# Loading projection weights and kept outputs one step ahead in a hybrid attention layer

## The chip, the cores and the metric

One Trainium2 chip, one core. The metric is device microseconds of one execution of the whole layer, as the median of several runs.

## The reference, cut to what matters

A streaming-encoder layer: 1024 tokens, width 1024, batch 1, float32. Its mixer runs eight heads of multi-head latent attention (MLA: low-rank latents, up projections to queries, keys and values, norms, rope) beside eight heads of chunked attention; one output projection takes both.

```python
q  = rmsnorm(q_lat, g_q) @ w_q_up                  # 256 -> 8 heads x 96
kv = rmsnorm(kv_lat, g_kv) @ w_kv_up               # 128 -> 8 heads x (64 keys + 64 values)
q, k = rmsnorm(q, g_mla_q), rmsnorm([k_nope, k_rope], g_mla_k)
o_mla = mla_attention(rope(q), rope(k), v)         # chunk-causal softmax
o_ca  = chunk_attention(cq, ck, cv, rel_bias)      # band of 9 chunks of 64
mixed = concat(o_mla, o_ca) @ w_out                # 1024 x 1024
x = x + g_a * mixed
x = x + g_m * (silu(gate) * val) @ w_down          # causal convolution and gated MLP, width 2816
```

## The kernel before

**Number form.** A float32 operand of a matrix product is kept as a high part in the matmul's own float32 form and a low remainder. One product is three matmuls: high x high (L150), high x low (L151), low x high (L152). So each weight that is loaded is *split*: a copy makes the high part (`hi_of`, L75, mostly on ACT), a subtraction the low part (`lo_of`, L82, on POOL or DVE).

**Stages.** Up to about 400 us the kernel does norms, input projection and the chunked heads; up to about 656 us the MLA heads' attention; to about 745 us the output projection, gated residual and norm; then the MLP.

**Units and fillers.** Attention is written as *units*: one head and one half of the tokens, eight tiles of 128 queries for both halves. The chunked heads have names with `c` (`Pc`, `hlc`, `PTc`, `pvc`), the MLA heads names with `m`. A tile's scores (L658) go through exp on ACT (L683, into `P`), the scaling to fp16 pairs on POOL (`hl`, L71) and DVE (L703), a DMA transpose issued by SP (`PT`, L705) and the values' matmuls (`pv`, L716). A finished half is scaled (`sb`, L723, and `o`, L724) and stored to `oT_d` in DRAM (L725). Between the tiles' steps the program takes pieces of a list of *fillers*, in this order: values and query/key projections of the chunked heads, `f_m` (the latents, tokens by tiles of 128), `f_up(0)` and `f_up(1)` (the up projections of the first and second four MLA heads) and `f_oca`. A pace (1.9 in chunked, 0.5 in MLA units) sets how much filler work follows each tile. `f_oca` multiplies the chunked heads' outputs, read back from `oT_d`, by their half of the output weights: two column halves n of 512, eight token tiles t in each; its results go to `part_d`. After the last unit, the other half of the output weights (rows 0 to 511, MLA) is loaded, and a loop over eight token tiles (`op` matmuls, kept outputs `ol`/`oh` L876, gate row `gabc` L872, stored partial sum `pa` L882 and L887, gate L888, residual add L889, `x1_d` L890) finishes the projection.

**Order.** All engines work their instructions in order. The order on each engine is decided at build time by the tile framework's scheduler, which runs its own model of the engines: an instruction written later moves ahead on its engine when its inputs and its buffer are free and the engine would be idle in the model. Scores, softmax and values have raised priority. So buffers decide how far ahead a load can be issued. SP issues all DMAs around the change, transposes included, in one queue.

**Buffers.** `qtile` gives one of two `sq` buffers (128 x 512 float32), `rtile` one of four `R` buffers. The chunked heads' values `vts` lie in six buffers of tag `v16`, which are free when the chunked units that read them are done. Split weights go to `G4`, eight buffers. In before:

- `f_up(gr)`: two query weights `wqr` (DMA L526) and the key/value weight `wkr` (L532) go through `sq` and are split to `wq`, `wk`; `wkj` (L535) is a sum of squares of it. Then for each token tile: `qu` matmuls, `uqr` (L553), `usq` (L555), `uss`, the power that makes the norm factor (L115, L116 on POOL), `qn` (L561), rope on POOL (L467 to L470); `ku` matmuls, `kraw` (L569), `vt` (L571, L572), `kss`, `kn` (L581, L582).
- `load_wo(k0, n, he, le)` (L586): four row blocks of the output weights for column half n, each loaded to `sq` (`wor`, L591) and split to `wo`. `f_oca` calls it for k0 = 4 at the start of each n; the line ahead of the projection calls it for k0 = 0 and both n, with the low part on POOL for n = 0 and on DVE for n = 1.
- `f_oca` loads a token block of kept outputs to `cl` (L604), copies the high part to `ch` and subtracts on POOL, and multiplies.

Of the kernel before, what the change touches and what calls it, by code (L numbers as in the profile page):

```python
# [12 lines left out]
F32 = mybir.dt.float32  # L13
# [49 lines left out]
def layer_kernel(ctx, tc, I, out):  # L63
# [3 lines left out]
    def f32(ap):  # L67
        return ap.bitcast(F32)
# [403 lines left out]
    def f_m():  # L472
        w = load_w("wm_", I["w_m"], NM)
        lat = {}
        for t in range(NT):
            h, j = divmod(t, 4)
            sl = slice(j * P, (j + 1) * P)
            pt = ps.tile([P, 512], F32, name=f"mp_{t}", tag="mm", bufs=2)
            yield from gemm3_f(pt[:, :NM], [(hT[k, h][:, 0, sl], hT[k, h][:, 1, sl]) + w[k] for k in range(ND)])
            raw = rtile(f"lat_{t}")  # L480
            act.activation(raw[:, :NM], pt[:, :NM], AF.Copy)
            sq = qtile(f"msq_{t}")
            ss = cst.tile([P, 2], F32, name=f"mss_{t}", tag="ss", bufs=4)
            r = cst.tile([P, 2], F32, name=f"mr_{t}", tag="rr", bufs=4)
            act.activation(sq[:, :QR], raw[:, :QR], AF.Square, accum_out=ss[:, 0:1])
            act.activation(sq[:, QR:QR + KVR], raw[:, QR:QR + KVR], AF.Square, accum_out=ss[:, 1:2])
            act.activation(sq[:, QR + KVR:NM], raw[:, QR + KVR:NM], AF.Square, accum_out=ssr[:, t:t + 1])
            pool.tensor_scalar(ss[:, 0:1], ss[:, 0:1], 1.0 / QR, EPS, op0=MUL, op1=ADD)
            rsqrt_mean(r[:], ss[:], KVR, cols=slice(1, 2))
            pool.tensor_scalar(raw[:, :QR], raw[:, :QR], r[:, 0:1], 1.0, op0=MUL, op1=MUL)  # L490
            pool.tensor_scalar(raw[:, QR:QR + KVR], raw[:, QR:QR + KVR], r[:, 1:2], 1.0, op0=MUL, op1=MUL)
            rope_apply(kr[:, t:t + 1, :], raw[:, QR + KVR:NM].unsqueeze(1), tabk, t, 1, raw[:, NM:NM + 64])
            lat[t] = raw
            if j == 3:
                for b in range(3):
                    ptt = ps.tile([P, 512], F32, name=f"lt_ps{h}_{b}", tag="T", bufs=TB)
                    for jj in range(4):
                        pe.transpose(ptt[:, jj * P:(jj + 1) * P], lat[4 * h + jj][:, b * P:(b + 1) * P], ident[:])
                    pg = pgtile([P, 2, 512], F32R, f"latT{h}_{b}")
                    gain = pk[:, C_GQL + b:C_GQL + b + 1]  # L500
                    act.activation(pg[:, 0], ptt[:], AF.Copy, scale=gain)
                    dve.scalar_tensor_tensor(pg[:, 1], ptt[:], gain, f32(pg[:, 0]), op0=MUL, op1=SUB)
                    latT[b, h] = pg
                    yield 436
# [9 lines left out]

    mq, mk, mv = {}, {}, {}

    def f_up(gr):
        if gr == 0:
            right.__exit__(None, None, None)
            for i in "4v3":  # L520
                G["cm" + i] = tc.tile_pool(name="gp" + i, bufs=1, side="right", reuse_waits="tile")
                G[i] = G["cm" + i].__enter__()
        wq = []
        for k in range(2):
            raw = qtile(f"wqr{gr}_{k}")
            sp.dma_start(raw[:, :384], I["w_qu"][gr][:, k, :])  # L526
            w = g4([P, 2, 512], F32R, f"wq{gr}_{k}")
            hi_of("a", w[:, 0, :384], raw[:, :384])
            lo_of("p", w[:, 1, :384], raw[:, :384], w[:, 0, :384])
            wq.append(w)  # L530
        raw = qtile(f"wkr{gr}")
        sp.dma_start(raw[:], I["w_kvu"][gr])  # L532
        ssw = cst.tile([P, 1], F32, name=f"sswm{gr}")
        junk = qtile(f"wkj{gr}")
        act.activation(junk[:, 0:256].rearrange("p (a b) -> p a b", a=4),  # L535
# [6 lines left out]
        for t in range(NT):  # L542
            h, j = divmod(t, 4)
            sl = slice(j * P, (j + 1) * P)
            if t % 2 == 0:
                mq[gr, t // 2] = g3([P, 2, 4, QK], F32, f"qn{gr}_{t}")
                mk[gr, t // 2] = g3([P, 2, 4, QK], F32, f"kn{gr}_{t}")
                mv[gr, t // 2] = G["v"].tile([P, 2, 4, 2, 64], F16, name=f"vt{gr}_{t}", tag="Gv", bufs=8)
            pt = ps.tile([P, 512], F32, name=f"qu{gr}_{t}", tag="mm", bufs=2)
            yield from gemm3_f(pt[:, :384], [(latT[k, h][:, 0, sl], latT[k, h][:, 1, sl], wq[k][:, 0, :384], wq[k][:, 1, :384])  # L550
                                for k in range(2)])
            raw = rtile(f"uqr{gr}_{t}")
            act.activation(raw[:, :384], pt[:, :384], AF.Copy)  # L553
            sq = qtile(f"usq{gr}_{t}")
            act.activation(sq[:, :384], raw[:, :384], AF.Square)  # L555
            ss = cst.tile([P, 4], F32, name=f"uss{gr}_{t}", tag="ss", bufs=4)
            r = cst.tile([P, 4], F32, name=f"ur{gr}_{t}", tag="rr", bufs=4)
            dve.tensor_reduce(ss[:], sq[:, :384].rearrange("p (a b) -> p a b", a=4), axis=AX.X, op=ADD)
            rsqrt_mean(r[:], ss[:], QK)
            q_t = mq[gr, t // 2][:, t % 2]  # L560
            dve.tensor_tensor(q_t, raw[:, :384].rearrange("p (a b) -> p a b", a=4),  # L561
                              r[:].unsqueeze(2).to_broadcast([P, 4, QK]), op=MUL)
            rope_apply(q_t[:, :, NOPE:], q_t[:, :, NOPE:], tabq, t, 4, raw[:, 0:256])
            pt = ps.tile([P, 512], F32, name=f"ku{gr}_{t}", tag="mm", bufs=2)
            yield from gemm3_f(pt[:], [(latT[2, h][:, 0, sl], latT[2, h][:, 1, sl], wk[:, 0], wk[:, 1])])
            p4 = pt[:].rearrange("p (a b) -> p a b", a=4)
            raw = rtile(f"kraw{gr}_{t}")
            r3 = raw[:, :256].rearrange("p (a b) -> p a b", a=4)
            act.activation(r3, p4[:, :, 0:NOPE], AF.Copy)  # L569
            v_t = mv[gr, t // 2][:, t % 2]  # L570
            act.activation(v_t[:, :, 0, :], p4[:, :, NOPE:], AF.Copy, scale=sc)  # L571
            dve.scalar_tensor_tensor(v_t[:, :, 1, :], p4[:, :, NOPE:], sc, v_t[:, :, 0, :], op0=MUL, op1=SUB)  # L572
            s3 = raw[:, 256:512].rearrange("p (a b) -> p a b", a=4)
            act.activation(s3, r3, AF.Square)
            ss = cst.tile([P, 4], F32, name=f"kss{gr}_{t}", tag="ss", bufs=4)
            r = cst.tile([P, 4], F32, name=f"kr{gr}_{t}", tag="rr", bufs=4)
            dve.tensor_reduce(ss[:], s3, axis=AX.X, op=ADD)
            pool.tensor_tensor(ss[:], ss[:], ssr[:, t:t + 1].to_broadcast([P, 4]), op=ADD)
            rsqrt_mean(r[:], ss[:], QK)
            k_t = mk[gr, t // 2][:, t % 2]  # L580
            dve.tensor_tensor(k_t[:, :, 0:NOPE], r3, r[:].unsqueeze(2).to_broadcast([P, 4, NOPE]), op=MUL)  # L581
            pool.tensor_tensor(k_t[:, :, NOPE:], kr[:, t:t + 1, :].to_broadcast([P, 4, ROPE]),  # L582
                               r[:].unsqueeze(2).to_broadcast([P, 4, ROPE]), op=MUL)


    def load_wo(k0, n, he, le):  # L586
        ws = []
        for k in range(k0, k0 + 4):
            raw = qtile(f"wor{k}_{n}")
            sl = slice(n * 512, (n + 1) * 512)  # L590
            sp.dma_start(raw[:], I["w_out"][k * P:(k + 1) * P, sl])  # L591
            w = g4([P, 2, 512], F32R, f"wo{k}_{n}")
            hi_of(he, w[:, 0], raw[:])
            lo_of(le, w[:, 1], raw[:], w[:, 0])
            ws.append(w)
        return ws

    def f_oca():
        for n in range(2):
            ws = load_wo(4, n, "a", "p")  # L600
            for t in range(NT):
                lo = rtile(f"cl{t}_{n}", (P, 4, P), F32R)
                hi = rtile(f"ch{t}_{n}", (P, 4, P), F32R)
                sp.dma_start(f32(lo[:]), oT_d[4:8, :, t * P:(t + 1) * P].rearrange("k p t -> p k t"))  # L604
                hi_of("a", hi[:], f32(lo[:]))
                lo_of("p", lo[:], f32(lo[:]), hi[:])
                pt = ps.tile([P, 512], F32, name=f"oc{t}_{n}", tag="mm", bufs=2)
                yield from gemm3_f(pt[:], [(hi[:, k], lo[:, k], ws[k][:, 0], ws[k][:, 1]) for k in range(4)])
                o = qtile(f"co{t}_{n}")
                act.activation(o[:], pt[:], AF.Copy)  # L610
                sp.dma_start(part_d[t][:, n * 512:(n + 1) * 512], o[:])


    def qk_page(src, name, rows, tag, bufs, gain):
# [218 lines left out]

    wo = [load_wo(0, n, "a", "v" if n else "p") for n in range(2)]
    att.__exit__(None, None, None)
    att_pg.__exit__(None, None, None)
    psA.__exit__(None, None, None)
# [312 lines left out]
```

## Time and profile before

| | us |
|---|---|
| median of three runs | 1465.47 |
| the three runs | 1463.65, 1468.99, 1465.47 |
| the profiled execution | 1464.36 |
| its span | 1462.2 |
| TensorE busy | 1278.0 (87%) |
| VectorE (DVE) busy | 1013.6 (69%) |
| GpSimd (POOL) busy | 823.0 (56%) |
| ScalarE (ACT) busy | 611.4 (42%) |

The mean granted clock of TensorE is 0.934 of full speed. Of the chain of work that ended last, 39% is PE, 17% DMA, 15% DVE and 13% POOL. Busy shares are means over all stages. In a line of the timeline the first number is the start in us, the second the length; `x3` is three instructions in a row, and brackets hold the engine's idle time just before and who ended it. `L82` is line 82 of the kernel. "SPq" is SP issuing a DMA; the data lands some microseconds later.

### The profile page before, as it was taken

The page shows a single profiled execution, that of the slowest core. Times are in us where ns is not written, and L with a number is a line of the kernel's source. Part 1 is how long each engine was busy: PE and PEld are TensorE (multiplying, and loading weights), DVE is VectorE, ACT ScalarE, POOL GpSimd, SP SyncE. Part 2 cuts the span into 40 slices and gives each one's busy share as a digit, 9 for nine tenths or more (in the row PEclk, how much of TensorE's full clock was granted, in tenths as well). Part 3 has the DMA queues.
Part 4 walks back from the last instruction along what each step waited for, and adds up shares of the span by engine and source line. Part 5 has one row for each costly group of instructions (what it writes and reads, how often), then busy time and mean ns, then how long its engine had stood idle before and what let it go on. Part 6 is the DMA issues. An engine that isn't in the chain of part 4 may idle for free.

```text
span 1462.2 us, 20198 instructions
## 1 busy us (share of the span) xinstructions
PE 1278.0 (87%) x6836; PEld 1058.7 (72%) x6836; DVE 1013.6 (69%) x1734; ACT 611.4 (42%) x1190; POOL 823.0 (56%) x845
## 2 busy tenths in 40 slices
PE   3859989998967788885776999999999998999997
PEld 2759878886756666664655878788888887887885
DVE  6874776476667868872476887777777777566653
ACT  4453354243455545543274434344444433332331
POOL 5263554274599954534644555566655555665662
PEclk9979987999787899996887999999999999999998
DMA  7323647455522577879611322322222244446442
GB/s 281 134 71 74 131 114 148 129 119 120 112 52 51 115 163 156 180 142 253 246 72 59 105 110 101 116 87 87 87 87 83 75 140 164 151 144 238 146 142 101
DMA packets 218595, 185.94 MB, mean 127 GB/s; under 512 B 148086, under 2 KB 183034, under 8 KB 217468
## 3 DMA queue, kind: packets, MB, share of 16 engines
q1 hardware_dynamic: 218492, 184.66, 44.5%
q8 instruction: 54, 0.88, 0.3%
q14 instruction: 49, 0.40, 0.1%
HBM read 121.17 MB, written 28.84 MB: 103 GB/s over the span
## 4 chain that ended last, share of the span: by engine, by line
PE 39%; DMA 17%; DVE 15%; POOL 13%; issue 12%; ACT 3%; SPq 1%; DVEq 0%; POOLq 0%; ACTq 0%
POOL wds L82 5%; DMA aw<-w_ada 5%; PE p L924 4%; PE p L926 4%; PE p L925 4%; DMA wu<-w_up 3%; DMA PTm<-hlm 3%; PE sc L658 2%; PE dnp L1067 2%; PE dnp L1069 2%; PE dnp L1068 2%; PE sm L658 2%; DVE adacc L243 2%; DVE aacc L430 1%; DVE u L1002 1%
## 5 line engine op out<-in xcount | busy, mean ns | idle before, releaser
L82 POOL TENSOR_TENSOR wds<-wd,wds 128x512 fp32r<-128x512 f32 x88 | 154.6, 1777 | 99.0 <-ACT wds L75 99.0
L82 POOL TENSOR_TENSOR wc<-ws,wc 128x512 fp32r<-128x512 f32 x22 | 65.4, 2972 | 137.8 <-ACT wc L75 137.8
L1057 DVE TENSOR_TENSOR wd<-wd,gmbc 128x1024 f32<-128x1024 f32 x44 | 67.5, 1533 | 80.4 <-DMA wd<-w_down 80.4
L1069 PE MATMUL dnp<-wds,g 128*128 128x512 f32 x308 | 118.4, 390 | 4.5 <-DVE g L82 4.5
L1067 PE MATMUL dnp<-wds,g 128*128 128x512 f32 x308 | 119.6, 390 | 1.9 <-DVE xo L1075 1.9
L75 ACT ACTIVATE wds<-wd 128x512 fp32r<-128x512 f32 x88 | 54.8, 624 | 157.3 <-PE dnp L1069 152.2
L1068 PE MATMUL dnp<-wds,g 128*128 128x512 f32 x308 | 119.5, 389 | 0.0
L71 POOL TENSOR_SCALAR hlm<-Pm,rim 128x512 f16<-128x512 f32 (+4 forms) x88 | 61.9, 706 | 70.1 <-DMA PTm<-hlm 55.1
L703 DVE SCALAR_TENSOR_TENSOR hlm<-Pm,rim,hlm 128x512 f16<-128x512 f32 (+4 forms) x88 | 68.0, 777 | 30.1 <-POOL hlm L71 29.7
L71 POOL TENSOR_SCALAR hlc<-Pc,ric 128x640 f16<-128x640 f32 (+2 forms) x64 | 45.3, 710 | 76.9 <-DVE ric L686 41.2
L1015 DVE TENSOR_TENSOR ws<-wu,wu 128x512 f32<-128x512 f32 x22 | 30.7, 1396 | 76.2 <-DMA wu<-w_up 76.2
L82 DVE TENSOR_TENSOR g<-gr,g 128x512 fp32r<-128x512 f32 x44 | 71.9, 1635 | 11.5 <-ACT g L75 11.5
L1001 DVE SCALAR_TENSOR_TENSOR u<-c,pk,u 128x1023 f32<-128x1023 f32 x44 | 77.4, 1765 | 2.0 <-ACT u L1000 2.0
L1036 ACT ACTIVATE u<-u 128x1024 f32<-128x1024 f32 x22 | 23.4, 1063 | 132.1 <-DVE u L1002 132.1
L683 ACT ACTIVATE Pc<-sc,mc 128x640 f32<-128x640 f32 (+2 forms) x64 | 42.1, 659 | 82.5 <-DVE mc L673 62.0
L658 PE MATMUL sm<-mk,mq 96*128 96x512 f32 (+3 forms) x288 | 68.9, 372 | 7.9 <-ACT Pm L683 7.3
L1000 ACT ACTIVATE u<-c,pk 128x1024 f32<-128x1024 f32 x44 | 52.3, 1236 | 56.2 <-DVE c L1032 56.2
L716 PE MATMUL pvm<-PTm,vt 128*128 128x128 f16 x576 | 50.5, 242 | 28.8 <-DMA PTm<-hlm 24.3
L658 PE MATMUL sc<-k,q 64*128 64x512 f32 (+3 forms) x288 | 70.3, 372 | 4.9 <-ACT Pc L683 3.0
L430 DVE SCALAR_TENSOR_TENSOR aacc<-aw,cs,aacc 128x256 f32<-128x256 f32 x84 | 44.9, 535 | 40.6 <-DMA aw<-w_ada 40.0
L716 PEld LDWEIGHTS <-vt 128*128 128x128 f16 x576 | 41.1, 109 | 41.7 <-issue 38.3
L1069 PEld LDWEIGHTS dnp<-wds,g 128*128 128x128 f32 x308 | 57.8, 188 | 17.7 <-DVE g L82 5.7
(368 smaller groups left out, 4342.0 us busy)
## 6 DMA issues: line engine op xcount, KB each, us to landing
wu<-w_up SPq DMA_DIRECT2D x44, 512.0 KB, 4.3
wd<-w_down SPq DMA_DIRECT2D x44, 512.0 KB, 4.7
aw<-w_ada SPq DMA_DIRECT2D x96, 128.0 KB, 2.3
g_d<-u SPq DMA_DIRECT2D x22, 512.0 KB, 2.6
gr<-g_d SPq DMA_DIRECT2D x44, 256.0 KB, 3.7
x<-x SPq DMA_DIRECT2D x16, 512.0 KB, 8.3
adaw<-w_ada_a SPq DMA_DIRECT2D x8, 1024.0 KB, 5.5
wq_r<-w_qk SPq DMA_DIRECT2D x32, 128.0 KB, 2.6
```

The source lines that it names most:

```text
L71: pool.tensor_scalar(o, i, s, 1.0, op0=MUL, op1=MUL)
L82: (pool if eng == "p" else dve).tensor_tensor(o, i, f32(hi), op=SUB)
L430: dve.scalar_tensor_tensor(acc[:], w[:], cs[:, k:k + 1], acc[:], op0=MUL, op1=ADD)
L658: last = pe.matmul(s[:, c:c + w], qpg[rs_, a, q], kpgs[kh][rs_, b, ko:ko + w], start=(a == 0 and b == 0), stop=(a == 1))
L703: dve.scalar_tensor_tensor(hl[:, w:2 * w], pp, ri[:], hl[:, :w], op0=MUL, op1=SUB)
L716: last = pe.matmul(u.pv[:, c], u.vst(j), mov, start=(x == 0), stop=(x == len(todo) - 1))
L924: pe.matmul(pt, sh, pg[:, 0], start=(k == 0), stop=False)
L1001: dve.scalar_tensor_tensor(u[:, 1:], c[:, :S - 1], pk[:, cv + 1:cv + 2], u[:, 1:], op0=MUL, op1=ADD)
L1057: dve.tensor_tensor(raw[:], raw[:], gmbc[:], op=MUL)
L1067: pe.matmul(pts[t][n], sh, w[n][:, 0], start=(j == 0), stop=False)
L1068: pe.matmul(pts[t][n], sh, w[n][:, 1], start=False, stop=False)
L1069: pe.matmul(pts[t][n], sl, w[n][:, 0], start=False, stop=(j == NF - 1))
```

## The change

Three loads move ahead, into new tiles (`vtile`) that take buffers of the tag `v16`:

- the raw up-projection weights of group 0 are fetched at token tile 4 of `f_m`, those of group 1 at tile 3 of `f_up(0)`;
- the output weights of the chunked heads' rows are fetched at tile 5 of `f_up(1)` (n = 0) and at step 2 of `f_oca` (n = 1, split at step 5); those of the MLA rows at step 2 of the second half of `f_oca` (n = 0, split at its step 5) and at its end (n = 1, split where `load_wo` was);
- `f_oca` runs one loop over 16 steps and asks for the next step's kept outputs ahead of a step's matmuls.

All loads, splits and matmuls stay the same in number and size. The low parts of the MLA rows' weights stay on POOL for n = 0 and on DVE for n = 1.

```diff
@@ f_m
             lat[t] = raw
+            if t == 4:
+                fetch_up(0)
...
+    def vtile(name):
+        return apg.tile([P, 512], F32, name=name, tag="v16", bufs=6)
+
+    def fetch_up(gr):
+        r = up_raw[gr] = [vtile(f"wqr{gr}_{k}") for k in range(3)]
+        for k in range(2):
+            sp.dma_start(r[k][:, :384], I["w_qu"][gr][:, k, :])
+        sp.dma_start(r[2][:], I["w_kvu"][gr])
...
@@ f_up
+        raws = up_raw.pop(gr)
         wq = []
         for k in range(2):
-            raw = qtile(f"wqr{gr}_{k}")
-            sp.dma_start(raw[:, :384], I["w_qu"][gr][:, k, :])
             w = g4([P, 2, 512], F32R, f"wq{gr}_{k}")
...
+            if t == 3 and gr == 0:
+                fetch_up(1)
+            if t == 5 and gr == 1:
+                fetch_wo(4, 0)
...
-    def load_wo(k0, n, he, le):
+    def fetch_wo(k0, n):
+        r = wo_raw[k0, n] = [vtile(f"wor{k}_{n}") for k in range(k0, k0 + 4)]
+        for i in range(4):
+            sp.dma_start(r[i][:], I["w_out"][(k0 + i) * P:(k0 + i + 1) * P, n * 512:(n + 1) * 512])
+
+    def split_wo(k0, n, he, le):
         ws = []
-        for k in range(k0, k0 + 4):
-            raw = qtile(f"wor{k}_{n}")
-            sl = slice(n * 512, (n + 1) * 512)
-            sp.dma_start(raw[:], I["w_out"][k * P:(k + 1) * P, sl])
-            w = g4([P, 2, 512], F32R, f"wo{k}_{n}")
+        for i, raw in enumerate(wo_raw.pop((k0, n))):
+            w = g4([P, 2, 512], F32R, f"wo{k0 + i}_{n}")
             hi_of(he, w[:, 0], raw[:])
             lo_of(le, w[:, 1], raw[:], w[:, 0])
             ws.append(w)
         return ws
 
     def f_oca():
-        for n in range(2):
-            ws = load_wo(4, n, "a", "p")
-            for t in range(NT):
...
+        ws = [split_wo(4, 0, "a", "p")]
...
+        lo = fetch(0)
+        for s in range(2 * NT):
+            n, t = divmod(s, NT)
+            hi = rtile(f"ch{t}_{n}", (P, 4, P), F32R)
+            hi_of("a", hi[:], f32(lo[:]))
+            lo_of("p", lo[:], f32(lo[:]), hi[:])
+            nxt = fetch(s + 1) if s + 1 < 2 * NT else None
+            if t == 2:
+                fetch_wo(4 * (1 - n), 1 - n)
...
+            if t == 5:
+                ws.append(split_wo(4 * (1 - n), 1 - n, "a", "p"))
+            lo = nxt
+        fetch_wo(0, 1)
+        wo.append(ws[2])
...
-    wo = [load_wo(0, n, "a", "v" if n else "p") for n in range(2)]
+    wo.append(split_wo(0, 1, "a", "v"))
```

More of the change, by code (lines that the diff above doesn't have):

```diff
@@ L522, in f_up @@
                 G[i] = G["cm" + i].__enter__()
+        raws = up_raw.pop(gr)
         wq = []
         for k in range(2):
-            raw = qtile(f"wqr{gr}_{k}")
-            sp.dma_start(raw[:, :384], I["w_qu"][gr][:, k, :])
             w = g4([P, 2, 512], F32R, f"wq{gr}_{k}")
-            hi_of("a", w[:, 0, :384], raw[:, :384])
-            lo_of("p", w[:, 1, :384], raw[:, :384], w[:, 0, :384])
+            hi_of("a", w[:, 0, :384], raws[k][:, :384])
+            lo_of("p", w[:, 1, :384], raws[k][:, :384], w[:, 0, :384])
             wq.append(w)
-        raw = qtile(f"wkr{gr}")
-        sp.dma_start(raw[:], I["w_kvu"][gr])
+        raw = raws[2]
         ssw = cst.tile([P, 1], F32, name=f"sswm{gr}")
@@ L598, in f_oca, with fetch @@
     def f_oca():
-        for n in range(2):
-            ws = load_wo(4, n, "a", "p")
-            for t in range(NT):
[L602 to L611, printed above, removed]
+        ws = [split_wo(4, 0, "a", "p")]
+        def fetch(s):
+            lo = rtile(f"cl{s}", (P, 4, P), F32R)
+            t = s % NT
+            sp.dma_start(f32(lo[:]), oT_d[4:8, :, t * P:(t + 1) * P].rearrange("k p t -> p k t"))
+            return lo
+        lo = fetch(0)
[7 more added lines that the diff above has]
+                fetch_wo(4 * (1 - n), 1 - n)
+            pt = ps.tile([P, 512], F32, name=f"oc{t}_{n}", tag="mm", bufs=2)
+            yield from gemm3_f(pt[:], [(hi[:, k], lo[:, k], ws[n][k][:, 0], ws[n][k][:, 1]) for k in range(4)])
+            o = qtile(f"co{t}_{n}")
+            act.activation(o[:], pt[:], AF.Copy)
+            sp.dma_start(part_d[t][:, n * 512:(n + 1) * 512], o[:])
+            if t == 5:
[3 more added lines that the diff above has]
+        wo.append(ws[2])
+    wo, wo_raw, up_raw = [], {}, {}
     def qk_page(src, name, rows, tag, bufs, gain):
```

## The prediction

> **What bounds the kernel now.** I read the page first: TensorE is busy 87% of the span, but that is a mean over stages, and the change touches only the stretch from about 385 us (end of the chunked heads) to 745 us (end of the output projection). So the next view was busy time per engine in 20 us stretches there; its columns are the stretch, its length, PE, weight loads, DVE, ACT and POOL busy (instructions in brackets), granted clock, DMA share, GB/s.
>
> ```profile
> 380.00:400.00 20.00, 17.47 (x114) 15.16 (x114) 14.94 (x43) 10.29 (x28) 13.14 (x21) 0.79 0.58 117
> 420.00:440.00 20.00, 11.34 (x42) 8.81 (x43) 12.96 (x39) 11.05 (x30) 18.94 (x42) 0.82 0.09 23
> 480.00:500.00 20.00, 13.94 (x91) 10.49 (x89) 16.94 (x44) 12.90 (x28) 19.14 (x33) 0.91 0.52 117
> 580.00:600.00 20.00, 16.98 (x127) 12.98 (x125) 17.19 (x44) 11.05 (x25) 13.20 (x15) 1.00 0.87 192
> 620.00:640.00 20.00, 16.75 (x111) 12.85 (x110) 15.73 (x37) 9.47 (x20) 8.09 (x11) 0.91 0.74 140
> 660.00:680.00 20.00, 6.95 (x60) 5.78 (x59) 5.97 (x11) 4.45 (x9) 8.85 (x9) 0.62 0.88 193
> ```
>
> From 400 to about 516 us POOL is full (18.6 to 19.1 of 20) and PE is not: rope, the norms' powers, the heads' scaling and the weight splits all queue on POOL. From 520 to 656 PE leads and POOL is half idle. From 660 to 680 nothing is busy: something is waited for. POOL's own waits between 403 and 516 us show the saturation best: this is all its idle time with a cause.
>
> ```profile
> POOL hlm L71 <- DMA PTm<-hlm: 0.6, 1, 0.6
> POOL cl L82 <- ACT ch L75: 0.6, 1, 0.6
> ```
>
> Next the raw output weights, `wor`: the durations of what reads them, and the idle time until they came.
>
> ```profile
> L82 POOL TENSOR_TENSOR wo<-wor,wo x12: 1261/1276/1844, 495.5 to 678.8; 128x512 fp32r<-128x512 f32 x12
>   DMA wor<-w_out: 22.9, 11
> ```
>
> They are waited for 11 times, because every raw weight of before takes one of the two `sq` buffers. The chain of waits shows where such a wait sets the time, at the second half's load and at the end of attention:
>
> ```profile
> 585.49 1.05 POOL cl L82
> 586.54 3.40 DMA wor<-w_out
> 589.97 0.64 ACT wo L75
> ...
> 673.05 3.27 DMA wor<-w_out
> 676.34 0.64 ACT wo L75
> 677.05 1.27 POOL wo L82
> 678.34 0.33 SPq L591
> 678.76 3.28 DMA ol<-oT_d
> 682.07 0.64 ACT oh L75
> ```
>
> Last, TensorE in the projection (start, length; in brackets its idle time and who ended it):
>
> ```profile
> 682.75 0.80 PE L150 MATMUL op<-wo,oh 128*128 128x512 f32 x1 [4.35 <-ACT oh L75]
> 708.96 0.80 PE L150 MATMUL op<-wo,oh 128*128 128x512 f32 x1 [6.53 <-ACT oh L75]
> 713.05 0.79 PE L152 MATMUL op<-wo,ol 128*128 128x512 f32 x1 [1.16 <-POOL ol L82]
> ```
>
> **Part 1, the end of attention (a gain).** No instruction is added or removed; the same 16 output-weight loads and splits move. In before ol0, the first load of kept MLA outputs, is issued at 678.76, behind a weight load that waits for a POOL split. In the changed order of instructions all weight loads lie before the last transposes, so SP reaches ol0 after the last one (673.73 + 1.25 = 674.98) and gabc (0.43): about 675.5, 3.3 us earlier. Its landing (3.28) now ends near 678.8, beside the last value matmuls (end 678.4). One ACT copy (0.69) stands first, then oh0 (0.64): op0 starts about 680. In before ops 0, 1 and 2 are interleaved, since the last four splits end only between 682.5 and 695.6; op0 ends at 699.3. In the changed order op0's 24 matmuls run alone: about 13 at the throttled step (0.43) and 11 at 0.23 = 8.1 us, so op0 ends about 688; op1 and op2 take 24 x 0.23 = 5.5 us each and end at 699. Before the dense run of op3 to op7 comes POOL's ol3 split, and on POOL it stands behind the add of op2's first half (in before op2's end 702.4, ol3's end 713.0: 10.6 us, with 3.2 us of the first add among it). That first add now runs at 691 to 694, so from op2 about 2.4 (DVE) + 2.4 (add) + 1.3 (ol3) = 6.1 plus steps: op3 at 705 to 706 instead of 713.05. That is **-7 us**; -4 if POOL's new queue (two up-weight splits, near 3 us each by the page's `wc` group, stand before ol3) eats half, -11 if the second idle gap shrinks too. From 713 on the sequence is dense and unchanged, so it carries through to the end.
>
> The stretch is half throttled: PE's step is 0.43 from 682.75 to 688.5 and again for 3 us after 713. The Trainium skill (TensorE: Matmul & The Clock Gate, "What's actually happening") says that about 3.4 us of steady work ends the throttle and an idle window of that length brings it back. The trace agrees with the order of size (5.8 and about 3.5 us); by that rule the gap before op3, still over 3.4 us, keeps its price and this part stays at -7.
>
> **Part 2, the second half's load (a small gain).** Wait 3.40 + ACT 0.64 + POOL 1.26 (at 582.98) are 5.3 us on the chain around 583 to 590, where PE keeps 16.98 of 20; in the three stretches from 600 to 660 it keeps 16.75 to 17.54. Attention units fill most of that wait, so I take **-2 us**, from 0 to -4.
>
> **Part 3, kept outputs one step ahead (nothing).** The scheduler of before already issues them ahead: two `cl` loads go out together at 510.29, before the store of the first result at 517.06; what holds each is a buffer of the four in `R`, released by the same matmuls in both orders. Cover: those four buffers. Without it the wait would be one landing, 3.1 us, per step.
>
> **Part 4, the hand-over to the up projections (a loss).** The early loads let the scheduler hoist splits. In the changed order POOL does, before the first power of up0 (403.10 in before): wq of both groups, both wk and the first two output weights, so two more wq (0.99 each), one wk (1.40) and two wo (1.28): 5.9 us more. POOL's idle gaps from 388 to 403 are 0.67 + 0.76 + 0.77 + 1.81 + 1.90 + 0.22 = 6.1 us, so in the best case it all fits. But engines work in order: on ACT the copies of wq, wk and two wo now stand before the last chunked exponential, each behind a landing (4.6 us wq, 2.9 wo), and then two latent copies before the first uqr copy; on PE the second qu stands behind the last chunked values; on SP five weight loads, each waiting for a POOL split, stand before the last chunked transposes. Chained by hand with these durations, the first power comes near 409, 6 us late. The stage then has 5.9 us less to split, but takes on the four second-half splits, 4 x 1.28 = 5.1 us, which before lay at 575 to 590 where POOL had time. So the full stage ends 6.3 - 5.9 + 5.1 = 5.5 us later; PE's later share of 16 to 17 in 20 absorbs about one: **+4.5 us**. From below: all fits and the stage ends 5.9 - 5.1 = 0.8 us earlier. From above: +9 with splits at their slowest (1.84 each: 7.4).
>
> The rows of the POOL split run from 1.26 to 1.84 us. The Trainium skill (GPSIMD Engine Reference, "Key points") says that GpSimd shares its SBUF interfaces with VectorE and contends with its two-input work. That speaks against moving splits to a stretch with DVE at 13 to 17 of 20; by the rule at its worst row this part is 2.3 us dearer.
>
> **Sum.** -7 - 2 + 0 + 4.5 = -4.5 against the profiled execution, which took 1464.36 us (span 1462.2 and 2.2 around it). It lies 1.1 us under the median of 1465.47, so on the median's scale the forecast is 1461.0. About 0.5% (7.3 us) is what a measurement here can tell from no change: faster begins at 1458.1, slower at 1472.8.
>
> **The rivals.**
> - *The hoisted splits fit POOL's gaps* (30%): the stage starts on time, -7 - 2 - 0.8 = -10, about 1455.5. For it: 6.1 us of gaps for 5.9 us of work. Against: they are gaps of an in-order engine that waited for ACT and DVE, and ACT gets new waits there.
> - *Slower: the in-order queues hold up the hand-over* (20%). Weight loads on SP and their copies on ACT before the last chunked softmax delay everything that POOL's full stage feeds on. It decides from the point where the first power of up0 is over 10 us late (after 413): then +10 - 5.9 + 7.4 (slow splits) = 11.5, with PE throttled in the gap (step 0.43 for 0.23 over some 6 us, +3) 14.5, less a tail of -5: +9.5, about 1475.
> - *Nothing arrives earlier than it mattered* (10%): the scheduler's look-ahead hid the loads and the POOL queue in the projection eats the tail; only ol0's 3.3 us are left, near 1462. Against: the 22.9 us of waits for `wor`.
> - The forecast (40%): 1461, its own range 1455 to 1468.
>
> **Chances.** Faster by over 0.5%: all of the first rival, a fifth of the forecast and of the third: 0.40. Slower: the second rival and a little of the forecast: 0.21. Within: 0.39. The range runs from just under the first rival, for the 4 us by which the tail is open, to the second: 1451 to 1474.
>
> **What would show it.** Right: ol0 issued near 675.5 on before's scale, op0 finished within 9 us of its start, no waits of ACT for `wor` after attention, POOL's first up0 power some 6 us later than 403 and its full stretch ending 4 to 6 us later. Wrong: a first power at or before 404 (first rival), or after 413 with PE gaps of several us between 390 and 415 (slower); or op3 not before 711 though ol0 came early.

## The result and the profile after

The changed kernel is slower: 1472.26 us in the median of 20 runs beside 1463.95 in 20 runs of the kernel before, a ratio of 1.0051 with a 95% interval of 1.0040 to 1.0062. By the ratio that is 7.5 us (the medians lie 8.3 us apart); the forecast was a gain of 4.5 us. The profiled execution is the shortest of the twenty (1465.34 us, span 1463.3), so a second profile of each kernel was taken on the chip of e5 to e8 (below, "again"; 1471.97 us before, 1479.76 us changed; the latter is longer than any of the twenty, so distances are read and not totals).

Where the time went is read from four distances in the trace. A: from the copy of the first latent transposition (ACT `latT`, a point that the change leaves alone) to the first up0 query copy (ACT `uqr`), the hand-over. B: on to the last `kn` on POOL, the up stage. C: on to the last value product, the rest of attention. D: on to the first product of the MLP, the tail. All are from start to start, in us.

| | A | B | C | D |
|---|---|---|---|---|
| before | 51.3 | 111.6 | 165.6 | 101.2 |
| before, again | 50.9 | 111.1 | 169.7 | 103.2 |
| changed | 63.9 | 109.8 | 164.9 | 96.6 |
| changed, again | 64.9 | 110.1 | 168.8 | 96.6 |

In the means the hand-over lost 13.3 us, the up stage won back 1.4, attention 0.8, and the tail won 5.6: 5.5 us later at the MLP, and no more after it (first MLP product to last down product 671.0 and 671.3 us before, 669.2 and 672.8 after). The other 2 us of the 7.5 are within what two profiles differ by.

The stretch from 400 to 420 of before, and the two from 380 on of the changed kernel (stretch, length, PE, weight loads, DVE, ACT, POOL, clock, DMA share, GB/s):

```profile
400.00:420.00 20.00, 15.24 (x80) 11.70 (x79) 15.26 (x41) 9.98 (x25) 18.62 (x33) 0.86 0.44 97
```

```profile
380.00:400.00 20.00, 16.05 (x81) 12.84 (x80) 13.02 (x41) 10.04 (x27) 14.96 (x22) 0.70 0.57 138
400.00:420.00 20.00, 11.45 (x62) 9.73 (x60) 12.20 (x26) 7.44 (x16) 10.63 (x15) 0.53 0.61 154
```

In before POOL worked 18.62 of 20 us from 400 to 420; now it works 10.63 and PE's granted clock falls to 0.53 (0.86 in before). From 420 on POOL is full again (18.50), and the stretches at 480 and 580 us look like before's. From 660 to 680 the changed kernel is still in its attention, whose last value product ends at 686.5 us and not at 678.4. POOL's waits from 403 to 526 us name the place: one of 9.0 us for DVE (it stands in brackets in the line at 415.11 below), where before's longest was 0.6 us.

What the change was meant to take away is gone: the waits for `wor` fell from 22.9 us to this, and the splits cost what they did.

```profile
L82 POOL TENSOR_TENSOR wo<-wor,wo x12: 1258/1285/1847, 400.7 to 585.9; 128x512 fp32r<-128x512 f32 x12
  DMA wor<-w_out: 1.4, 2
```

POOL at the hand-over, one line of before and then the changed kernel, shows why the full stretch starts late:

```profile
387.39 0.48 POOL L490 TENSOR_SCALAR lat<-lat,mr 128x256 f32<-128x256 f32 x1
```

```profile
391.91 1.26 POOL L82 TENSOR_TENSOR wk<-wqr,wk 128x512 fp32r<-128x512 f32 x1
...
396.96 1.00 POOL L82 TENSOR_TENSOR wq<-wqr,wq 128x384 fp32r<-128x384 f32 x1
...
399.30 1.44 POOL L82 TENSOR_TENSOR wk<-wqr,wk 128x512 fp32r<-128x512 f32 x1
400.69 1.85 POOL L82 TENSOR_TENSOR wo<-wor,wo 128x512 fp32r<-128x512 f32 x1
402.51 0.65 POOL L490 TENSOR_SCALAR lat<-lat,mr 128x256 f32<-128x256 f32 x1
...
415.11 0.20 POOL L115 TENSOR_SCALAR uss<-uss 128x4 f32<-128x4 f32 x1 [9.03 <-DVE uss L571]
```

L490 scales the last latent tile. In before it ran at 387.39, ahead of every split; now it stands behind seven of them, and with it wait its transposition, the latent copies on ACT and, behind these in ACT's order, the first `uqr` copy. So POOL held up the work that feeds POOL.

In the tail the first projection step starts 2.6 us after the last value product instead of 4.35, and the fourth step's dense run 29.8 us after that product's end (686.54) instead of 34.7 (678.39):

```profile
689.14 0.80 PE L150 MATMUL op<-wo,oh 128*128 128x512 f32 x1 [2.60 <-ACT oh L75]
710.62 0.50 PE L150 MATMUL op<-wo,oh 128*128 128x512 f32 x1 [1.78 <-ACT oh L75]
716.33 0.80 PE L152 MATMUL op<-wo,ol 128*128 128x512 f32 x1 [2.40 <-POOL ol L82]
```

### The profile page after: what moved, and what is told of

It reads as the page before. It is cut to its first block, busy times and chain, and to the rows that moved or that the text cites. A ratio compares the mean times of both kernels' runs of the same rounds, so it can differ in the third digit from the quotient of the medians.

```text
span 1463.3 us, 20189 instructions
## 1 busy us (share of the span) xinstructions
PE 1280.7 (88%) x6836; PEld 1058.0 (72%) x6836; DVE 1016.9 (69%) x1734; ACT 611.4 (42%) x1190; POOL 822.4 (56%) x845
## 4 chain that ended last, share of the span: by engine, by line
PE 37%; DMA 17%; POOL 15%; DVE 15%; issue 11%; ACT 2%; SPq 1%; DVEq 0%; POOLq 0%; ACTq 0%
DMA aw<-w_ada 6%; POOL wds L82 5%; PE p L955 4%; PE p L957 4%; PE p L956 4%; DMA wu<-w_up 3%; PE sc L689 2%; DMA PTm<-hlm 2%; PE dnp L1098 2%; PE dnp L1100 2%; PE dnp L1099 2%; PE sm L689 2%; DVE aacc L430 2%; DVE adacc L243 2%; DMA cl<-oT_d 1%
## 5 line engine op out<-in xcount | busy, mean ns | idle before, releaser
L71 POOL TENSOR_SCALAR hlm<-Pm,rim 128x512 f16<-128x512 f32 (+4 forms) x88 | 65.0, 741 | 64.5 <-DMA PTm<-hlm 43.3
L1100 PEld LDWEIGHTS dnp<-wds,g 128*128 128x128 f32 x308 | 57.8, 188 | 17.0 <-DVE g L82 5.0
L1098 PEld LDWEIGHTS dnp<-wds,g 128*128 128x128 f32 x308 | 57.8, 188 | 15.0 <-DVE xo L1106 2.2
```

What stands on the lines that cost most here:

```text
L71: pool.tensor_scalar(o, i, s, 1.0, op0=MUL, op1=MUL)
L1098: pe.matmul(pts[t][n], sh, w[n][:, 0], start=(j == 0), stop=False)
L1100: pe.matmul(pts[t][n], sl, w[n][:, 0], start=False, stop=(j == NF - 1))
```

## The experiments

Each kernel ran beside the kernel before on one chip. The experiments used four chips (e1 to e4; e5 to e8; e9 and e10; e11 to e13), with before's median from 1466.1 to 1469.5 us, so ratios to it are given, with their 95% intervals. Distances come from one profile of each.

### The parts of the change by themselves

**e1**: before with the tail part alone.

```diff
...
+                if n == 1 and t == 2:
+                    fetch_wo(0, 0)
...
+                if n == 1 and t == 5:
+                    wo.append(split_wo(0, 0, "a", "p"))
+        fetch_wo(0, 1)
...
-    wo = [load_wo(0, n, "a", "v" if n else "p") for n in range(2)]
+    wo.append(split_wo(0, 1, "a", "v"))
```

> The kernel before with one part of the change: the MLA rows' output weights go through the v16 buffers and are fetched and split during the last part of the filler, all else through the two sq buffers. Theory 1 (the hand-over to the up projections costs, the tail gains): first power of up0 at 403 as in before, first load of kept MLA outputs about 3 us earlier, the main run of the fourth projection step 5 to 7 us earlier, median 1457 to 1459 beside 1464 of before. Rival (the tail's gain is lost again in the MLP): same steps early, but the median at 1463 to 1465.

Measured: 1.0005 (0.9985 to 1.0025). The tail is there (D 94.6), the hand-over as in before (A 50.2), but C is 176.8: the gain is given back, and in attention, not in the MLP as the rival had it. Two units are slow. One, which ends at 505.2, takes 16.1 us instead of 10.2 and 10.5; it is slow in e7 and e8 too (see e8). The other, which ends at 615.8, takes 23.1 us where before's takes 14.5 and 16.5. POOL there:

```profile
591.37 0.69 POOL L71 TENSOR_SCALAR hlm<-Pm,rim 128x512 f16<-128x512 f32 x1 [1.75 <-DMA PTm<-hlm]
592.02 5.40 POOL L82 TENSOR_TENSOR wo<-wor,wo 128x512 fp32r<-128x512 f32 x4
597.41 0.58 POOL L71 TENSOR_SCALAR hlm<-Pm,rim 128x384 f16<-128x384 f32 x1
```

Four splits in a row stand between two scalings of the softmax. By e7, where POOL keeps one split at this place and DVE has four, the first is the filler's own and the others are MLA rows' weights, some 50 us before the step at which the code asks for them. That a `G4` buffer coming free let them go there is not shown.

**e2**: before with the early up weights alone.

```diff
+            if t == 4:
+                fetch_up(0)
...
+            if t == 3 and gr == 0:
+                fetch_up(1)
```

> The kernel before with one part of the change: only the raw up-projection weights go through the v16 buffers and are fetched early. Theory 1 (POOL splits that are hoisted ahead of the last latent tile delay the hand-over): first power of up0 at 410 to 414 instead of 403, end of attention 6 to 9 us later, median 1470 to 1473. Rival 2 (the second half's output-weight splits inside POOL's full stretch are what costs): first power may be late, but the median stays at 1462 to 1466, since those splits stay at their old place here.

Measured: 1.0127 (1.0098 to 1.0157), some 18 us, more than theory 1 expected (6 to 9 in the median); A 66.2, first power at 422.6, D 102.5. Rival 2 fell.

**e3**: the full change with the up weights back in `sq`.

```diff
-                fetch_up(0)
...
+            raw = qtile(f"wqr{gr}_{k}")
+            sp.dma_start(raw[:, :384], I["w_qu"][gr][:, k, :])
...
```

> The changed kernel with its up-projection weights put back into the two sq buffers; all output weights keep the v16 buffers, so the eight splits for the chunked rows still move into POOL's full stretch. Theory 1: first power of up0 back at 403, end of attention 0 to 3 us later than before, tail 5 us shorter, median 1459 to 1462. Rival 2: the end of attention stays some 8 us late and the median at 1470 to 1473.

Measured: 1.0019 (0.9998 to 1.0041). A is 50.7 (the first power is at 408.0 because everything from the first latent on is 5.5 us later), B 114.8, C 170.7, D 95.5. The hand-over is repaired by the up weights alone. The splits that moved into the full stretch cost some 3.5 us in B, and the end of attention and the median came later than theory 1 had them.

### What holds up the hand-over

**e4**: the full change, the low parts of the up weights and of the first four output weights on DVE.

```diff
-            lo_of("p", w[:, 1, :384], raws[k][:, :384], w[:, 0, :384])
+            lo_of("v", w[:, 1, :384], raws[k][:, :384], w[:, 0, :384])
...
-        ws = [split_wo(4, 0, "a", "p")]
+        ws = [split_wo(4, 0, "a", "v")]
```

> The changed kernel with the low parts of the up weights and of the first four output weights computed on DVE instead of POOL; loads, buffers and ACT copies stay early. Theory 1a (POOL's queue ahead of the last latent tile is the cause): the last latent tile is scaled on POOL some 10 us earlier, first power of up0 at 403 to 407, median 1457 to 1463. Rival 1b (the loads on SP and the copies on ACT ahead of the last chunked softmax are the cause): first power stays after 411 and the median at 1469 to 1473.

Measured: A 53.1, so 11 us of the delay are gone as 1a says; by the clock of the whole the first power is at 412.6, since its first latent copy is at 355.5. But the ratio is 1.0047 (1.0031 to 1.0064): C is 175.6. Why attention is dearer in this order was not found.

**e9**: e2 with the splits on DVE, a cleaner pair.

```diff
-            lo_of("p", w[:, 1, :384], raws[k][:, :384], w[:, 0, :384])
+            lo_of("v", w[:, 1, :384], raws[k][:, :384], w[:, 0, :384])
...
-        lo_of("p", wk[:, 1], raw[:], wk[:, 0])
+        lo_of("v", wk[:, 1], raw[:], wk[:, 0])
```

> The kernel with only the up-projection weights fetched early, which measured 1.0127 of before, with one edit: the low parts of these weights on DVE instead of POOL. The orders of the two kernels are the same up to the last latent tile. Theory 1a (six splits on POOL ahead of the last latent tile's scaling): from the first latent transposition's copy to the first up0 query copy 51 to 55 us instead of 66, and a ratio of 0.998 to 1.004. Rival 1b (loads on SP and copies on ACT): still over 60 us, ratio over 1.009.

Measured: 1.0060 (1.0039 to 1.0080) against 1.0127; A 55.9 against 66.2. Both lie a little above what theory 1a expected and well below the rival's. The three ACT lines of each are the first latent copy, the last latent tile and the first query copy, of "before, again", e2 and e9:

```profile
351.93 0.69 ACT L501 ACTIVATE latT<-lt_ps,pk 128x512 fp32r<-128x512 f32 x1
...
385.62 0.52 ACT L481 ACTIVATE lat<-mp 128x416 f32<-128x416 f32 x1 [1.24 <-PE mp L152]
...
402.80 0.49 ACT L553 ACTIVATE uqr<-qu 128x384 f32<-128x384 f32 x1 [0.67 <-PE qu L152]
```

```profile
353.02 0.68 ACT L503 ACTIVATE latT<-lt_ps,pk 128x512 fp32r<-128x512 f32 x1
...
393.57 0.51 ACT L481 ACTIVATE lat<-mp 128x416 f32<-128x416 f32 x1
...
419.23 0.49 ACT L566 ACTIVATE uqr<-qu 128x384 f32<-128x384 f32 x1
```

```profile
351.46 0.68 ACT L503 ACTIVATE latT<-lt_ps,pk 128x512 fp32r<-128x512 f32 x1
...
392.15 0.51 ACT L481 ACTIVATE lat<-mp 128x416 f32<-128x416 f32 x1
...
407.36 0.49 ACT L566 ACTIVATE uqr<-qu 128x384 f32<-128x384 f32 x1 [1.21 <-PE lt_ps L500]
```

From the last latent tile to the first query copy: 17.2, 25.7 and 15.2 us. That half is the splits on POOL. From the first latent copy to the last latent tile: 33.7, 40.6 and 40.7 us. That half, 7 us, is not: it is late before any split. In the changed kernel it is 39.6 and 40.5, so its 13 us are about 6 and 7.

The trace tells what that first half is made of. Of "changed, again", the last latent product on PE and the exponential on ACT that follows:

```profile
390.39 0.35 PE L152 MATMUL mp<-wm_h,hT 128*128 128x416 f32 x1
...
392.49 0.80 ACT L714 ACTIVATE Pc<-sc,mc 128x640 f32<-128x640 f32 x1 [4.68 <-DVE mc L704]
```

On PE the last latent product ends 37.2 and 38.0 us after the first latent copy (both profiles), in before 34.2 and 33.7: 36 score and 43 or 44 value matmuls of the chunked heads are recorded between the two, in before 24 and 24. On ACT its copy, at 393.28 here, then comes 2.4 to 2.5 us after the product's end, behind that exponential, which waited for DVE; in before it follows at once.

**e11, e12, e13**: the side work's weight loads `aw` were the suspect for the first half, since with early up weights two more of them stand ahead of the chunked transposes on SP. These kernels leave out the last 14 and so leave part of one modulation vector incomplete: before, the full change, and e9.

```diff
-                for k in range(ND):
+                for k in range(ND if (m, n) not in ((4, 2), (4, 3)) else 1):
```

> The kernel before without the last 14 of the 96 side loads aw and their products (two column blocks of one modulation vector are left incomplete). If the aw chain holds up the hand-over in before too, from the first latent transposition's copy to the last latent copy takes 24 to 31 us instead of 34, and the ratio is 0.992 to 0.998; if it is hidden, 33 to 35 us and 0.998 to 1.001.

> The changed kernel with the same 14 side loads left out. Theory (6 us of the late hand-over from the aw chain, 7 from the splits on POOL): the last latent copy comes at the same distance as in the cut kernel before, within 2 us, instead of 6 us later; the first up0 query copy still 6 to 9 us later than there. Rival (the 6 us come from something else that moved): the last latent copy still 5 us or more later than in the cut kernel before.

> The kernel with early up weights and their low parts on DVE, with the same 14 side loads left out. Theory: neither cause is left, the first up0 query copy comes at the same distance as in the cut kernel before, within 3 us, and the time within 0.2% of that kernel's. Rival: hand-over still 5 us late.

Measured: from the first latent copy to the last latent tile 37.6, 36.6 and 38.5 us; A 53.1, 60.3 and 52.6; ratios to before 1.0056 (1.0032 to 1.0080), 1.0106 (1.0068 to 1.0143) and 1.0005 (0.9986 to 1.0024). The first half became the same in all three, as expected, but at 36.6 to 38.5 us and not under 34: before got slower without the loads, which neither case for e11 had. So the waits for `aw` are not shown to be the cause. What moved is the order of the last latent product among the chunked heads' work: 36 score and 44 value matmuls stand ahead of it in e11 to e13 too, 36 and 42 to 44 in e2, e4 and e9, and 24 and 24 in e1, e3 and e8. Early up weights go with the late place, but e11 has it without them; what makes the scheduler choose it is open. The second half is confirmed once more: with the splits on POOL 7.2 us more in A than e11, on DVE 0.5 less. The times of e11 and e13 differ by 0.5% all the same, 5 us of it in B: equal hand-overs do not make equal kernels.

### Whether the tail's gain can be kept

**e5, e6**: both kernels once more.

> The kernel before, profiled once more on the chip of these runs, to see how much its stages vary. If the attention stage is steady, from the last key norm of the up stage to the last value product takes 163 to 168 us as in the first profile (165.6), and its units' distances repeat within 2 us; then the 176.8 us of the run with the tail alone is an effect of the edit. If it varies by itself, 172 to 178 us shows here too.

> The changed kernel, profiled once more. The first profile was of its fastest execution of twenty (1465.3 beside a median of 1472.3). Theory (hand-over): the first up0 query copy again comes 11 to 15 us later after the first latent transposition's copy than in before (63 to 66 us instead of 51), the attention units from 590 to 620 us again hold a slow one (19 us or more), and the slower total lies in one of these two. Rival: the extra 7 us of the usual execution lie before 350 us or in the MLP, where nothing was changed.

Measured: 169.7 us of attention in e5, above the 163 to 168 and below e1's 176.8, the units repeating within 2 us; so one kernel's C varies by some 4 us, and e1's loss is more than that. In e6 A is 64.9, the unit around 619 to 628 us takes 19.4 us (19.5 in the first profile). Both expected places hold; the extra 14.6 us of this execution's span over the first profile's are spread (5.2 before the first latent copy, 3.9 in C, most of the rest in the MLP), so for them the rival was half right.

**e7**: e1 with the low parts of the burst on DVE.

```diff
-                    wo.append(split_wo(0, 0, "a", "p"))
+                    wo.append(split_wo(0, 0, "a", "v"))
```

> The kernel with the tail part alone, its first four MLA-row output weights with their low parts on DVE instead of POOL. Theory 3 (a burst of four splits on POOL ahead of the softmax scaling delays a unit in mid-attention and gives back what the tail gains): the slow unit near 592 to 616 us shrinks from 23 to 14 to 17 us, last value product to last projection matmul stays at 59 to 60 us, ratio 0.995 to 0.998. Rival (DVE is as loaded as POOL there, so the place of the burst matters and not its engine): unit still over 20 us, ratio 0.999 to 1.003.

Measured: 0.9995 (0.9976 to 1.0014); the unit takes 18.4 us, C is 168.3 instead of 176.8, D 95.6. So with the low parts off POOL that unit is 4.7 us shorter, and still longer than before's; the unit that is slow near 505 us in e1 is so here (15.8 us). The time did not fall beyond its interval: neither case is borne out on the whole.

**e8**: only the second column half early.

```diff
...
+        fetch_wo(0, 1)
...
-    wo = [load_wo(0, n, "a", "v" if n else "p") for n in range(2)]
+    wo.append(load_wo(0, 0, "a", "p"))
+    wo.append(split_wo(0, 1, "a", "v"))
```

> The kernel before with only the second column half of the MLA rows' output weights fetched ahead through the v16 buffers; the first half goes through the sq buffers at the end as in before, so no split moves into mid-attention. Theory 3: units as in before (no unit over 18 us from 580 to 620 us), the first projection step runs alone, last value product to last projection matmul 59 to 61 us instead of 64, ratio 0.995 to 0.998. Rival (the tail's gain is not real in the usual execution): ratio 0.999 to 1.001.

Measured: 1.0021 (1.0004 to 1.0039), a miss. No burst is left, D is 98.6, but C is 173.9, and a unit near 500 us takes 16.0 instead of 10.2 and 10.5; the one that ends at 615.2 takes 18.8, over the 18 expected, without any burst. The mere use of the `v16` buffers had moved other instructions; on SP a weight load that waits for a split now stands ahead of a transpose:

```profile
502.10 5.53 SPq L595 DMA_DIRECT2D wor<-w_out  x2
507.72 3.30 SPq L724 DMA_TRANSPOSE PTm<-hlm  x2
```

In e5 the load at this place is one and takes 0.70 us. In e1 and e7 the two loads stand there as well (5.54 and 5.55 us), in the unit that is slow.

**e10**: the second half into the attention's page buffers, which come free only at the end.

```diff
-    wo = [load_wo(0, n, "a", "v" if n else "p") for n in range(2)]
+    wo = [load_wo(0, 0, "a", "p")]
+    raws = []
+    for i in range(2):
+        pgt = pgtile([P, 2, 512], F32, f"wor1p{i}")
+        for j in range(2):
+            k = 2 * i + j
+            sp.dma_start(pgt[:, j], I["w_out"][k * P:(k + 1) * P, 512:1024])
...
+        lo_of("v", w[:, 1], raw, w[:, 0])
```

> The kernel before with one edit at its end: the second column half of the MLA rows' output weights is loaded into the page buffers of the attention (tag pg) instead of the two sq buffers, so it need not wait for the splits of the first half; every engine's order up to the last unit is that of before. Theory 3 (the tail's gain is real and was given back in mid-attention, where the v16 buffers changed the order): up to the end of attention as in before, last value product to last projection matmul 58 to 61 us instead of 64 to 66.6, ratio 0.995 to 0.998. Rival (the gain is lost behind the projection): the same early end of the projection, but ratio 0.999 to 1.001.

Measured: 0.9965 (0.9953 to 0.9977), 1462.1 us beside 1468.15. The interval lies clear of 1, though the gain is under the 0.5% that the prediction took for telling. A, B and C are before's (49.9, 111.5, 167.9), D is 98.8, and the fourth step starts 30.8 us after the last value product:

```profile
680.36 1.01 PE L716 MATMUL pvm<-PTm,vt 128*128 128x128 f16 x8 [2.04 <-DMA PTm<-hlm]
687.22 0.79 PE L150 MATMUL op<-wo,oh 128*128 128x512 f32 x1 [5.85 <-ACT oh L75]
712.20 0.79 PE L152 MATMUL op<-wo,ol 128*128 128x512 f32 x1 [3.30 <-POOL ol L82]
```

The first step even starts later than in the changed kernel (5.85 us of idle PE, not 2.60); the last split of an output weight ends at 685.7 us, before it, where in before it ends at 696.0, so the first steps need not wait for splits in their midst. The last product to the last projection matmul is 62.1 us, a little over what was expected.

## Why the prediction was wrong

- **Part 4, the hand-over, is the step that failed.** It was right in kind (hoisted splits, in-order engines), and too small: it set the first power 6 us late; counted from the first latent copy it came 14 and 16 us late. About 7 us are POOL's splits, as e9 shows. The sum looked for room for their 5.9 us in POOL's idle gaps from 388 us on, behind the last latent tile's scaling (387.39 in before), and its chain to 409 names copies on ACT, products on PE and loads on SP, but not that scaling; in the changed kernel seven splits stand ahead of it (402.51). About 6 us more are the last latent product's own new place behind the chunked heads' work, to which the sum gave nothing. What moved that product is open.
- The two other terms of Part 4 came out near their prices. The stage was to have 5.9 us less to split and to take on 5.1: B fell by 1.4 for the 0.8 of this difference. Apart, e3 shows +3.5 for the 5.1, and e2, which moves the up weights' splits alone (two wq and one wk, 3.4 at the sum's prices), shows -2.4. So of the 10 us between the forecast -4.5 and the +5.5 found at the MLP, 7.4 are Part 4's: 13.3 - 1.4 = 11.9 for +4.5.
- **Part 1, the tail**, was right in kind and somewhat large: -5.6 in D for -7. What its own -4 case named came in part. On POOL, which is not idle from 708.7 to 716.3 us, two splits of the MLP's weights (at 692.95 and 694.19 in before) and an add now stand ahead of the fourth step's low part (715.01), for which the dense run waits:

```profile
709.27 1.27 POOL L82 TENSOR_TENSOR wa<-wu,wa 128x512 fp32r<-128x512 f32 x1
710.50 2.24 POOL L82 TENSOR_TENSOR wb<-wu,wb 128x512 fp32r<-128x512 f32 x1
712.70 2.35 POOL L920 TENSOR_TENSOR x<-x,pa 128x1024 f32<-128x1024 f32 x1
```

- Not priced at all: the new place of the first four MLA-row splits. They were taken to be free where POOL is half idle. In e1 a burst of them cost its unit 4.7 us (against e7), since in an in-order queue it is not spread over the idle time. In the changed kernel they are no burst (570.2, 572.7, 583.7 and 585.9 us), and the unit from 599 to 619 us, with no such split in it, still takes some 4 us more than before's (19.5 and 19.4); e7 and e8 have such a unit too. What makes it slow is open.
- **Part 2** (-2) is not seen: C changed by 0.8, and that is within what one kernel's C varies by. **Part 3** (nothing) met no contrary run, and was not tried by itself.
- The rival on the slower side was what happened. Its condition, a first power after 413, was met (415.1 and 421.5), with PE throttled as it said (granted clock 0.53); its price of +9.5 is near the 7.5 measured. That it came so near is partly luck: its cause, loads on SP and copies on ACT, is at most the lesser part, since e9 moved only the low parts to DVE and took 10 of the 15 us out.
- The prediction cites the Trainium skill (GPSIMD Engine Reference, "Key points"): GpSimd shares its SBUF interfaces with VectorE and contends with VectorE work that has two SBUF inputs. The splits of output weights on POOL took 1258 to 1847 ns after and 1261 to 1844 before, so the move made them no dearer here.

## What to carry to other kernels

Where a scheduler hoists whatever has its buffer and its inputs, a prefetch into free buffers moves not the load alone: its copies and splits come along, in bursts, ahead of work that others wait for, and the line in the code where it is asked for does not hold them back. Price such a change on the in-order queue that takes the follow-up work, and look at the order from well before the first moved instruction. A buffer that comes free late (e10) is a way of saying "not before this point", and kept all of the order that was good.

## What the runs showed of the hardware that was not expected

How long a 256 KB load of kept outputs takes from its issue to its landing differed with the time of its issue. In the changed kernel's tail one took 8.46 us (issued at 703.46 us) and a later one 2.77 us (724.54); the DMA share was 0.93 from 700 to 720 us and 0.39 from 720 to 740. In before it was 6.41 us (699.81) and 2.89 us (719.80), at shares of 0.76 and 0.44. Which of the loads beside it make it long was not tried.
